# A SwiGLU feed-forward whose up products are formed as 7 half-size block products, with the down products in a stage of their own

## The chip, the cores and the metric

The kernel runs on 1 core of one Trainium2 chip. The metric is the device time of one execution in microseconds (us). The time before is 2326.37 us, the median of 3 runs (2324.08, 2326.37 and 2328.72).

## What is computed

One layer of a hybrid encoder on 1152 tokens (1024 of a prompt, 128 of 8 running streams): retention and differential attention, merged and projected, and then a feed-forward with a residual. The change touches the feed-forward and the stages just ahead of it:

```python
h = h + merged @ W_o
x2 = rmsnorm(h, norm2_g)
g, u = split(x2 @ w_ffn_up)          # 1024 -> 2 x 2816
h = h + (silu(g) * u) @ w_ffn_down   # 2816 -> 1024
y = rmsnorm(h, normf_g)
```

All values are float32. The kernel splits each operand of a product into a high part h, rounded by a cast, and a low part l, the difference, and sums three products, high x high, high x low and low x high (`mm3`, L82).

## The kernel before

Tokens are held in 9 blocks of 128, in three tiles of 384. The feature axis of 1024 has 8 slices of 128 (`KT`). The last stages are these.

- The branch product (`pdb`, weights w_db) writes the merged vector as MH and ML, three tiles each.
- The output projection `proj(b, half)` (tiles `pe`, 24 matmuls of 512 columns) adds the residual into H, which stays in SBUF for all 9 blocks. `norm2(b)` forms the norm, and `turn2()` transposes it (tiles `pte`) into X2H and X2L.
- The feed-forward runs over 22 slices f of 128 hidden features. `split_w` (L188) loads one block of weights (512 KB), casts the high part on ScalarE and forms the low part on VectorE, each 128x512 or 128x1024. `ffn_dense` (L1277) makes 24 matmuls of 384 columns for each of the three token tiles: 72 for a gate block (`pg`), 72 for an up block (`pu`). ScalarE applies Silu to the gate (L1291); VectorE multiplies the up product into it (L1374), ScalarE casts (L1375) and GpSimd forms the low part (L1376).
- After each pair of slices, `down(fs_, acts, final)` makes 12 matmuls of 512 columns for each of 9 token blocks (`pd`, two halves, two slices): 108 matmuls. VectorE adds each result into H (L1393). The last call also forms the final norm and stores the output.

Every load and store is issued by SyncE (`load` L73, `store` L76), in the order of its queue. The instructions of one engine run in the order in which the program lists them; the order around the feed-forward comes from the tile framework's scheduling of this code.

```python
for p_ in range(NF // 2):
    pair = (2 * p_, 2 * p_ + 1)
    last = p_ == NF // 2 - 1
    acts = [up(pair[0])]
    if last:
        down(*prev, False)
    acts.append(up(pair[1]))
    if prev is not None and not last:
        down(*prev, False)
    prev = (pair, acts)
```

Of the kernel before, what the change touches and what calls it, by code (L numbers as in the profile page):

```python
# [19 lines left out]
P = 128  # L20
# [10 lines left out]
KT = 8  # L31
# [31 lines left out]
def tile_kernel(ctx, tc, I, O):  # L63
# [15 lines left out]
    def mm(out, l, r, start, stop):  # L79
        nc.tensor.matmul(out, l, r, start=start, stop=stop)  # L80
# [8 lines left out]
    wp = pool(ctx, "wp", 2)  # L89
# [122 lines left out]
    vecd = dr.tile([DH, VL], F, name="vecd", tag="vecd")  # L212
    skd = [dr.tile([P * (VL + 1)], F, name=f"skd{h}", tag=f"skd{h}") for h in range(DH)]
# [1004 lines left out]
    xstack.close()  # L1218


    mstack = ExitStack()
    mp = pool(mstack, "mp", 3)
    MH = [mp.tile([P, KT, 384], R, name=f"MH{c}", tag="MH") for c in range(3)]
    ML = [mp.tile([P, KT, 384], R, name=f"ML{c}", tag="ML") for c in range(3)]
    wo0 = ExitStack()
    wop = pool(wo0, "wo0", 1)

    def split_w_o(pool_, half, kp, raw_pool=None):
        raw = (raw_pool or wp).tile([P, 1024], F, name=f"wo{half}{kp}w", tag="wr", bufs=1)
# [8 lines left out]
    wo_0 = []  # L1238
    with ExitStack() as st:
        yp = pool(st, "dy", 1, None, "right")  # L1240
        tp = pool(st, "dt", 4, None, "right")
        YD = [[yp.tile([P, KT, 384], R, name=f"YD{i}{c}", tag=f"YD{i}{c}") for c in range(3)] for i in range(2)]
        for c in range(3):
            load_split(YD[0][c], YD[1][c], yd[c])
        for n in range(KT):
            w = split_w(wp, I["w_db"][n], f"db{n}")
            for c in range(3):
# [10 lines left out]

                def evac(c, ps):
                    nc.vector.tensor_tensor(gt, ps, gt, op=ALU.mult)  # L1260
                    nc.gpsimd.tensor_tensor(mt, mt, gt, op=ALU.add)  # L1261

                for _ in dense_c(w, YD, c, 0, evac, f"pdb{n}"):
                    pass
                nc.scalar.copy(MH[c][:, n, :], mt)
                nc.vector.tensor_tensor(ML[c][:, n, :], mt, MH[c][:, n, :].bitcast(F), op=ALU.subtract)
            if n >= KT - 4:
                wo_0.append(split_w_o(wop, 0, n - KT + 4, tp))


    hstack = ExitStack()
    hp = pool(hstack, "hp", 1, None, "right")
    H = hp.tile([P, 9, 1024], F, name="H", tag="H")
    fs = pool(hstack, "fs", 2, None, "right")
    X2H, X2L = [None] * 3, [None] * 3

    def ffn_dense(w, evac, name):  # L1277
        h, l = w
        for c in range(3):
            ps = psum("dq", f"{name}_{c}")  # L1280
            for k in range(KT):
# [12 lines left out]
    with ExitStack() as st:  # L1294
        wo1 = pool(st, "wo1", 1, None, "right")
        ep = pool(st, "ep", 2, None, "right")
        g2 = ep.tile([P, 1024], F, name="g2", tag="g2", bufs=1)
        load(g2, I["norm2_g"].broadcast_to([P, 1024]))
        wo = (wo_0, [split_w_o(wo1, 1, kp) for kp in range(4)])
        w_g0 = split_w(wp, I["w_up"][0], "wg0")  # L1300

        def proj(b, half):
            c, j = b // 3, b % 3
# [3 lines left out]
            load(xt, I["x_all"][r0:r1, hs])  # L1307
            ps = psum("m", f"pe{b}_{half}")
            for k in range(KT):
                h, l = wo[half][k // 2]  # L1310
                a = slice(j * P, (j + 1) * P)
                mh, ml = MH[c][:, k, a], ML[c][:, k, a]
                mm(ps, mh, h[:, k % 2, :], k == 0, False)
                mm(ps, mh, l[:, k % 2, :], False, False)
                mm(ps, ml, h[:, k % 2, :], False, k == KT - 1)
            nc.vector.tensor_tensor(H[:, b, hs], ps, xt, op=ALU.add)
# [3 lines left out]
        def norm2(b):  # L1320
            c = b // 3
            if b % 3 == 0:
                X2H[c] = mp.tile([P, KT, 384], R, name=f"X2H{c}", tag="MH")
                X2L[c] = mp.tile([P, KT, 384], R, name=f"X2L{c}", tag="ML")
            turns.append(norm_to_T(ep, H[:, b, :], b, P, g2, X2H[c], X2L[c], (b % 3) * P, "e"))
# [209 lines left out]
```

## Time and profile before

| what | value |
|---|---|
| median of the runs | 2326.37 us |
| the profiled execution | 2326.88 us |
| its span, first to last instruction | 2325.0 us |
| TensorE busy | 2288.9 us, 98% |
| VectorE busy | 968.5 us, 42% |
| ScalarE busy | 762.6 us, 33% |
| GpSimd busy | 502.9 us, 22% |
| moved by DMA | 200.01 MB, mean 86 GB/s |
| mean granted clock of TensorE | 0.998 of 2.4 GHz |

The profile shows one execution. Busy time of an engine off the chain costs nothing by itself; the chain that ended last shows which work set the end. PE is TensorE, DVE VectorE, ACT ScalarE, POOL GpSimd and SP SyncE.

### The profile page before, as it was taken

What the parts mean: (1) busy time and instruction counts of PE and PEld (TensorE: products, weight loads), DVE (VectorE), ACT (ScalarE), POOL (GpSimd) and SP (SyncE); (2) the same over time, 40 slices, a digit from 0 to 9 for tenths busy, and PEclk for the clock granted to TensorE, in tenths of its full rate; (3) what the DMA queues carried; (4) which work ended last, traced back from release to release, by engine and by line L of the source; (5) the groups of instructions that cost most, each with busy time, mean ns of one, the idle gap of its engine ahead of it and who ended that gap; (6) DMA issues with size and microseconds to landing.
All of it is one profiled execution on the core that took longest, in us unless ns stands there. A gap on an engine that the chain in (4) does not pass through costs nothing.

```text
span 2325.0 us, 34635 instructions
## 1 busy us (share of the span) xinstructions
PE 2288.9 (98%) x13738; PEld 2186.9 (94%) x13738; DVE 968.5 (42%) x2248; ACT 762.6 (33%) x1756; POOL 502.9 (22%) x591
## 2 busy tenths in 40 slices
PE   8999999999999999999999999999999999999998
PEld 8999999999999999999899998899999999999987
DVE  5353333434556555654442433323323342233345
ACT  4233223134555555555544322221121112111112
POOL 2132212133323332332434320010100011000101
PEclk9999999999999999999999999999999999999999
DMA  6422322234233232322428532111110111101112
GB/s 213 129 85 70 105 73 96 85 100 145 77 91 91 79 98 88 96 80 88 138 89 265 160 119 93 37 37 46 55 46 31 42 46 55 36 29 46 55 37 91
DMA packets 129362, 200.01 MB, mean 86 GB/s; under 512 B 13432, under 2 KB 97656, under 8 KB 129200
## 3 DMA queue, kind: packets, MB, share of 16 engines
q1 hardware_dynamic: 129200, 197.80, 27.1%
q8 instruction: 108, 1.77, 0.3%
q14 instruction: 54, 0.44, 0.1%
HBM read 148.76 MB, written 53.78 MB: 87 GB/s over the span
## 4 chain that ended last, share of the span: by engine, by line
PE 90%; DVE 4%; DMA 2%; ACT 2%; issue 1%; POOL 1%; SPq 0%; DVEq 0%; POOLq 0%; ACTq 0%
PE pu L80 12%; PE pg L80 12%; PE pd L80 11%; PE ddv L80 4%; PE ddk L80 4%; PE pdb L80 4%; PE pe L80 4%; PE drv L80 4%; PE dgd L80 4%; PE dgr L80 4%; PE drg L80 4%; PE ddq L80 3%; PE po L80 3%; PE psc L80 3%; PE drb L80 3%; PE drk L80 2%
## 5 line engine op out<-in xcount | busy, mean ns | idle before, releaser
L1376 POOL TENSOR_TENSOR afl<-sgf,afh 128x384 fp32r<-128x384 f32 x66 | 70.1, 1062 | 729.8 <-ACT afh L1375 729.8
L1393 DVE TENSOR_TENSOR H<-pd,H 128x512 f32<-128x512 f32 x198 | 136.2, 690 | 109.6 <-PE pd L80 109.6
L915 DVE CUSTOM_DVE_ANT_0 E<-psc,TB 128x144 f32<-128x144 f32 (+6 forms) x224 | 113.0, 507 | 112.5 <-PE psc L80 106.3
L1291 ACT ACTIVATE sgf<-pg 128x384 f32<-128x384 f32 x66 | 32.3, 489 | 313.9 <-PE pg L80 313.9
L894 ACT ACTIVATE E<-E,ng 128x272 f32<-128x272 f32 (+7 forms) x128 | 101.0, 789 | 47.1 <-DVE ng L920 44.0
L1374 DVE TENSOR_TENSOR sgf<-pu,sgf 128x384 f32<-128x384 f32 x66 | 36.7, 556 | 169.1 <-PE pu L80 169.1
L80 PE MATMUL psc<-K,QH 128*128 128x144 f32 (+6 forms) x224 | 73.3, 330 | 6.9 <-DVE mx L915 5.2
L1375 ACT CAST afh<-sgf 128x384 fp32r<-128x384 f32 x66 | 33.7, 511 | 117.0 <-DVE sgf L1374 116.9
L80 PE MATMUL psc<-K,QL 128*128 128x144 f32 (+6 forms) x224 | 71.1, 319 | 0.0
L975 DVE TENSOR_TENSOR al<-pa,ah 128x512 fp32r<-128x512 f32 (+1 forms) x80 | 46.4, 582 | 43.8 <-ACT ah L974 42.9
L904 DVE SCALAR_TENSOR_TENSOR E<-E,rt,E 128x144 f32<-128x144 f32 (+3 forms) x64 | 54.7, 855 | 0.0
L80 PEld LDWEIGHTS psc<-K,QH 128*128 128x128 f32 x224 | 42.2, 188 | 10.4 <-issue 5.5
L566 POOL TENSOR_TENSOR v<-V,v 128x256 fp32r<-128x256 f32 x36 | 27.0, 749 | 113.4 <-ACT v L565 113.4
L792 DVE SCALAR_TENSOR_TENSOR QL<-ddq,QH 64x384 fp32r<-64x384 f32 (+1 forms) x48 | 24.5, 510 | 57.5 <-ACT QH L786 54.9
L974 ACT CAST ah<-pa 128x512 fp32r<-128x512 f32 (+1 forms) x80 | 40.2, 503 | 23.5 <-PE pa L963 23.2
L963 PE MATMUL pa<-ident,E 128*128 128x128 f32 x288 | 44.6, 272 | 0.0
L1261 POOL TENSOR_TENSOR mt<-mt,gt 128x384 f32<-128x384 f32 x24 | 24.4, 1017 | 83.0 <-DVE gt L1260 70.4
L80 PEld LDWEIGHTS psc<-K,QL 128*128 128x128 f32 x224 | 42.3, 189 | 0.0
L532 ACT COPY V<-drv 128x256 f32<-128x256 f32 x36 | 13.4, 372 | 83.9 <-PE drv L80 83.9
L80 PE MATMUL po<-al,VH 128*128 128x256 f32 x128 | 36.4, 284 | 1.8 <-DVE al L975 1.7
L963 PEld LDWEIGHTS pa<-ident,E 128*128 128x128 f32 x288 | 35.1, 140 | 2.2
L620 POOL TENSOR_TENSOR Sp<-S,Sp 128x256 fp32r<-128x256 f32 x32 | 23.9, 747 | 60.1 <-ACT Sp L619 52.2
(1774 smaller groups left out, 8064.7 us busy)
## 6 DMA issues: line engine op xcount, KB each, us to landing
skd<-vecd SPq DMA_DIRECT2D x8, 584.0 KB, 13.0
out_k_t<-kf SPq DMA_DIRECT2D x8, 584.0 KB, 3.3
xt<-in_x_all SPq DMA_DIRECT2D x9, 512.0 KB, 5.4
vd<-v SPq DMA_DIRECT2D x36, 128.0 KB, 1.7
yr<-SG SPq DMA_DIRECT2D x24, 192.0 KB, 1.8
gd<-gdt SPq DMA_DIRECT2D x24, 192.0 KB, 1.8
gr<-grt SPq DMA_DIRECT2D x24, 192.0 KB, 1.8
YRL<-yr SPq DMA_DIRECT2D x12, 384.0 KB, 5.0
```

What stands on the lines that cost most here:

```text
L80: nc.tensor.matmul(out, l, r, start=start, stop=stop)
L894: nc.scalar.activation(E[m][:, :nk], E[m][:, :nk], AF.Exp, bias=ng[:, m : m + 1], accum_out=sm[:, m : m + 1])
L904: nc.vector.scalar_tensor_tensor(E[0][:, :nk], E[1][:, :nk], rt[:, 0:1], E[0][:, :nk], op0=ALU.mult, op1=ALU.add)
L915: nc.vector.tensor_tensor_reduce(out=E[m][:, k0:k1], in0=ps, in1=TB[:, u0 : u0 + k1 - k0], scale=1.0, scalar=-3e38, op0=ALU.add, op1=ALU.m ...
L963: nc.tensor.transpose(pt[:, o : o + P], blk[2 * g + j][:, NM + P * t : NM + P * (t + 1)], ident)
L974: nc.scalar.copy(ah[:, :o], pt[:, :o])
L975: G.later(LAT["ah"], lambda ah=ah, al=al, pt=pt, o=o: nc.vector.tensor_tensor(al[:, :o], pt[:, :o], ah[:, :o].bitcast(F), op=ALU.subtract))
L1291: nc.scalar.activation(sg[:, 384 * c : 384 * (c + 1)], ps, AF.Silu)
L1374: nc.vector.tensor_tensor(sg[:, cs], ps, sg[:, cs], op=ALU.mult)
L1375: nc.scalar.copy(ah[:, cs], sg[:, cs])
L1376: nc.gpsimd.tensor_tensor(al[:, cs], sg[:, cs], ah[:, cs].bitcast(F), op=ALU.subtract)
L1393: nc.vector.tensor_tensor(H[:, b, hs], ps, H[:, b, hs], op=ALU.add)
```

## The change

**Gate and up products.** The weights w_up are taken in 22 groups of two blocks, with the features in two halves k (512 each) and the tokens in two halves t (576 each). The first group (gate of slices 0 and 1) is formed as before, by `dense_gate`, 72 matmuls of 384 columns for each block. In the other 21 groups, the 2x2 block product over (two weight blocks) x (two halves of k) x (two halves of t) is formed from 7 products in place of 8. A product is 4 slices x 3 matmuls for each of two column ranges of 288. The products are taken in the order 1, 6, 2, 7, 5, 4, 3. The sums of weight blocks for products 5, 6, 7 and 3 (S) are made by GpSimd, and their high and low parts by ScalarE and VectorE (`w_group`, `halves`). The sums of token operands for products 7, 5, 6 and 4 (T, high and low, 4 slices x 576) are made once, in three thirds of 4 x 192 elements, after the last transpose. The results are put together in PSUM and in `s1`, `U2` and `U3`.

**Activations and H through DRAM.** The finished activations of two slices are stored to `actd`, and H to `hd`; both are read back later.

**Down products.** They are a stage of their own: three passes over three token blocks. In a pass, 6 PSUM banks hold the sums over all 22 slices; each slice loads its w_down block (512 KB) and 128x384 activations (192 KB), casts and splits them, and makes 18 matmuls of 512 columns. H is read back and added at the end of a pass. In the last pass the three last slices are taken block by block.

**Around it.** MH and ML are one tile each, and take the transposed norm as well. The weights of the branch product are split in 512-wide halves, from a pool of 8 buffers with two raw buffers.

```diff
+    hd = [dr.tile([P, 1024], F, name=f"hd{b}", tag=f"hd{b}") for b in range(9)]
+    actd = [dr.tile([P, NTOK], F, name=f"act{f}", tag=f"act{f}") for f in range(NF)]
...
+    ORDER = "1627543"
...
+            sums = {
+                "6": ((s1, a21, a22, ALU.add), (s2, s1, a11, ALU.subtract)),
+                "7": ((s3, a11, a21, ALU.subtract),), "3": ((s4, a12, s2, ALU.subtract),),
+            }
+            src = {"1": a11, "2": a12, "4": a22, "5": s1, "6": s2, "7": s3, "3": s4}
+            for p in ORDER:
+                for o, a, b, op in sums.get(p, ()):
+                    nc.gpsimd.tensor_tensor(o, a, b, op=op)
+                (W[p],) = halves(src[p], f"wu{g}_{p}", None, 1)
+                yield
...
+            key = {"1": "A", "2": "A", "6": "B", "7": "D", "4": "D", "5": "C", "3": "C"}[p]
+            s_ = st_[c]
+            new = key not in s_
+            if new:
+                s_[key] = fpsum(f"{name}{key}{c}")[:, :288]
+            ps, (ah, al), (bh, bl) = s_[key], W[p], XO[p]
+            cs = slice(288 * c, 288 * (c + 1))
+            for k in range(4):
                 ks = slice(k * P, (k + 1) * P)
-                mm3(ps[:, :384], h[:, ks], l[:, ks], X2H[c][:, k, :], X2L[c][:, k, :], k == 0, k == KT - 1)
-            evac(c, ps[:, :384])
-            yield
-
-    def gate_f(f, w):
-        sg = fs.tile([P, NTOK], F, name=f"sgf{f}", tag="sgf")
-
-        def ev_g(c, ps):
-            nc.scalar.activation(sg[:, 384 * c : 384 * (c + 1)], ps, AF.Silu)
-        return sg, ffn_dense(w, ev_g, f"pg{f}")
-
-    with ExitStack() as st:
-        wo1 = pool(st, "wo1", 1, None, "right")
-        ep = pool(st, "ep", 2, None, "right")
+                mm(ps, ah[:, ks], bh[:, k, cs], new and k == 0, False, not new)
+                mm(ps, al[:, ks], bh[:, k, cs], False, False, not new)
+                mm(ps, ah[:, ks], bl[:, k, cs], False, k == 3, not new)
...
+            if p == "1":
+                s_["s1"] = tmp("s1")
+                nc.scalar.copy(s_["s1"], ps)
+            elif p == "2":
+                evac(0, 0, c, ps, None)
+            elif p == "6":
+                s_["U2"] = tmp("U2")
+                nc.vector.tensor_tensor(s_["U2"], ps, s_["s1"], op=ALU.add)
+            elif p == "7":
+                s_["U3"] = tmp("U3")
+                nc.vector.tensor_tensor(s_["U3"], ps, s_["U2"], op=ALU.add)
+            elif p == "5":
+                evac(1, 1, c, ps, s_["U3"])
+            elif p == "4":
+                evac(1, 0, c, ps, s_["U2"])
+            else:
+                evac(0, 1, c, ps, s_["U2"])
...
+    dense_gate(0, 0)
+    turn2()
+    dense_gate(0, 1)
+    dense_gate(0, 2)
...
+            def out(p, eng):
+                h, l = (a[:, :, cs] for a in T[p])
+                nc.scalar.copy(h, t[p])
+                sub(l, t[p], h.bitcast(F), eng)
+            def between(p, a, b, eng):
+                t[p], d = new("d"), new("e")
+                sub(t[p], a[0], b[0], eng)
+                sub(d, a[1], b[1], eng)
+                sub(t[p], t[p], d, eng, ALU.add)
+            def less(p, a, u, eng):
+                t[p] = new("f")
+                sub(t[p], a[0], u, eng)
+                sub(t[p], t[p], a[1], eng, ALU.add)
+            between("5", x[0, 1], x[0, 0], nc.gpsimd)
+            less("6", x[1, 1], t["5"], nc.vector)
+            out("6", nc.vector)
+            out("5", nc.vector)
+            between("7", x[1, 1], x[0, 1], nc.gpsimd)
+            out("7", nc.vector)
+            t6 = t["6"]
+            t["4"] = t6
+            sub(t["4"], x[1, 0][0], t6, nc.vector)
+            sub(t["4"], t["4"], x[1, 0][1], nc.vector, ALU.add)
+            out("4", nc.vector)
...
+    Wg, st_g = w_group(NF // 2)
+    for n in range(2):
+        for c in range(3):
+            if n:
+                dense_gate(n, c)
+                next(st_g, None)
...
+    def ev_up(n, t, c, ps, u):
+        o = sg[n][:, 576 * t + 288 * c : 576 * t + 288 * (c + 1)]
+        if u is None:
+            nc.vector.tensor_tensor(o, ps, o, op=ALU.mult)
+        else:
+            v = up_.tile([P, 288], F, name=f"v{n}{t}{c}", tag="v", bufs=2)
+            nc.vector.tensor_tensor(v, ps, u, op=ALU.add)
+            nc.gpsimd.tensor_tensor(o, v, o, op=ALU.mult)
...
+    def w_down(p_, f):
+        w = halves(raw_w(I["w_down"][f], f"wd{p_}_{f}"), f"wd{p_}_{f}")
+        raw = fp.tile([P, 384], F, name=f"ar{p_}_{f}", tag="ar", bufs=2)
+        load(raw, actd[f][:, 384 * p_ : 384 * (p_ + 1)])
+        ah = fp.tile([P, 384], R, name=f"ah{p_}_{f}", tag="ah")
+        al = fp.tile([P, 384], R, name=f"al{p_}_{f}", tag="al")
+        nc.scalar.copy(ah, raw)
+        nc.gpsimd.tensor_tensor(al, raw, ah.bitcast(F), op=ALU.subtract)
+        return w, ah, al
...
+        strassen(W, XO, ev_up if u else ev_gate, nxt, f"f{i}")
+        if u:
+            for n in range(2):
+                store(actd[2 * p_ + n], sg[n])
...
-            def ev_u(c, ps):
-                cs = slice(384 * c, 384 * (c + 1))
-                nc.vector.tensor_tensor(sg[:, cs], ps, sg[:, cs], op=ALU.mult)
-                nc.scalar.copy(ah[:, cs], sg[:, cs])
-                nc.gpsimd.tensor_tensor(al[:, cs], sg[:, cs], ah[:, cs].bitcast(F), op=ALU.subtract)
...
+        for p_ in range(3):
+            ps = {(b, half): fpsum(f"pd{p_}_{b}_{half}") for b in range(3) for half in range(2)}
+            hr = []
+            for b in range(3):
+                hr.append(yp.tile([P, 1024], F, name=f"hr{p_}_{b}", tag="hr", bufs=4))
+                load(hr[b], hd[3 * p_ + b])
+            def block(b, f, w, ah, al):
                 bs = slice(b * P, (b + 1) * P)
                 for half in range(2):
+                    (wh, wl), o = w[half], ps[b, half]
+                    mm(o, ah[:, bs], wh, f == 0, False)
+                    mm(o, ah[:, bs], wl, False, False)
+                    mm(o, al[:, bs], wh, False, f == NF - 1)
+            ops = w_down(p_, 0)
+            late = []
+            for f in range(NF):
+                now = ops
+                if f + 1 < NF:
+                    ops = w_down(p_, f + 1)
+                if p_ == 2 and f >= NF - 3:
+                    late.append((f, *now))
+                else:
+                    for b in range(3):
+                        block(b, f, *now)
...
-                    ps = psum(("m", "tr")[half], f"pd{fs_[0]}_{b}_{half}")
-                    for i, ((wh, wl), (ah, al)) in enumerate(zip(ws, acts)):
-                        mm(ps, ah[:, bs], wh[:, hs], i == 0, False)
-                        mm(ps, ah[:, bs], wl[:, hs], False, False)
-                        mm(ps, al[:, bs], wh[:, hs], False, i == len(ws) - 1)
-                    nc.vector.tensor_tensor(H[:, b, hs], ps, H[:, b, hs], op=ALU.add)
```

On GpSimd, between the last transposes and the first group of 7 products, the rows before are the low parts of activations (afl); those of the change are the sums of token operands. td and te are what T5 and T7 are formed in, S is a tile of weight sums, wu1 a pair of raw weight blocks, sg a gate tile.

```order
L114 TENSOR_TENSOR re7r<-re7t,mhalf 128x1
L114 TENSOR_TENSOR re8r<-re8t,mhalf 128x1
L1376 TENSOR_TENSOR afl_16642<-sgf_16483,afh_16641 128x384 x3
L1376 TENSOR_TENSOR afl_16821<-sgf_16741,afh_16820 128x384 x3
L1376 TENSOR_TENSOR afl_17000<-sgf_16920,afh_16999 128x384 x3
L1376 TENSOR_TENSOR afl_17179<-sgf_17099,afh_17178 128x384 x3
```

Now, same engine, from the second third of the sums to the first products of the first group (the six operations of a third stand ahead in the same pattern):

```order
L1465 TENSOR_TENSOR td_16762<-MH 128x768
L1465 TENSOR_TENSOR td_16762<-td_16762,te_16763 128x768
L1465 TENSOR_TENSOR te_16774<-ML 128x768
L1465 TENSOR_TENSOR td_16773<-MH 128x768
L1465 TENSOR_TENSOR td_16773<-td_16773,te_16774 128x768
L1465 TENSOR_TENSOR te_16786<-ML 128x768
L1322 TENSOR_TENSOR S_16949<-wu1bw 128x512
L1322 TENSOR_TENSOR S_16949<-wu1aw,wu1bw 128x512
L1322 TENSOR_TENSOR S_16949<-S_16949,wu1aw 128x512
L1322 TENSOR_TENSOR S_16949<-wu1aw,S_16949 128x512
L1465 TENSOR_TENSOR td_16785<-MH 128x768
L1465 TENSOR_TENSOR td_16785<-td_16785,te_16786 128x768
```

The four weight sums of the second group (S) have come to stand between the last T7 operation te and its td; all of this is new on GpSimd.

On VectorE at the same place, rows that did not exist before, up to the low part of the last third of T6 (last row; T_16629 is the low tile of T6, T_16627 of T5, T_16625 of T7, T_16631 of T4):

```order
L1465 TENSOR_TENSOR T_16629<-tf_16755,T_16628 128x4x192
L1465 TENSOR_TENSOR T_16625<-td_16762,T_16624 128x4x192
L1465 TENSOR_TENSOR tf_16755<-MH,tf_16755 128x768
L1465 TENSOR_TENSOR tf_16755<-tf_16755,ML 128x768
L1236 TENSOR_TENSOR wu_3l_16909<-S_16827,wu_3h_16908 128x512
L1465 TENSOR_TENSOR T_16627<-td_16773,T_16626 128x4x192
L1465 TENSOR_TENSOR T_16631<-tf_16755,T_16630 128x4x192
L1236 TENSOR_TENSOR wu_1l_16951<-wu1aw,wu_1h_16950 128x512
L1465 TENSOR_TENSOR tf_16778<-MH,td_16773 128x768
L1465 TENSOR_TENSOR tf_16778<-tf_16778,ML 128x768
L1465 TENSOR_TENSOR T_16629<-tf_16778,T_16628 128x4x192
```

Each row waits for the one ahead, so the last T6 comes behind T7 and T4 of the second third and two weight differences.

On SyncE, the loads of the feed-forward before, in the stretch of slices 4 to 9 (wg and wu are blocks of w_up, wd of w_down):

```order
L74 DMA wd4w<-in_w_down 128x1024
L74 DMA wd5w<-in_w_down 128x1024
L74 DMA wg8w<-in_w_up 128x1024
L74 DMA wu8w<-in_w_up 128x1024
L74 DMA wg9w<-in_w_up 128x1024
L74 DMA wu9w<-in_w_up 128x1024
```

And in the first down pass of the change (ar is the activation tile):

```order
L74 DMA ar_17_22594<-act_189 128x384
L74 DMA wd_18w<-in_w_down 128x1024
L74 DMA ar_18_22628<-act_190 128x384
L74 DMA wd_19w<-in_w_down 128x1024
L74 DMA ar_19_22662<-act_191 128x384
L74 DMA wd_20w<-in_w_down 128x1024
```

One w_down block and one activation tile stand for each slice, in each of three passes; before, each w_down block was loaded once, among four blocks of w_up a pair.

## Rows read from the trace of the kernel before

**Rows 1.** The page: span, busy time of TensorE, and the chain by line.
```profile
span 2325.0 us, 34635 instructions
PE 2288.9 (98%) x13738; PEld 2186.9 (94%) x13738; DVE 968.5 (42%) x2248; ACT 762.6 (33%) x1756; POOL 502.9 (22%) x591
...
PE pu L80 12%; PE pg L80 12%; PE pd L80 11%; PE ddv L80 4%; PE ddk L80 4%; PE pdb L80 4%; PE pe L80 4%; PE drv L80 4%; PE dgd L80 4%; PE dgr L80 4%; PE drg L80 4%; PE ddq L80 3%; PE po L80 3%; PE psc L80 3%; PE drb L80 3%; PE drk L80 2%
```

**Rows 2.** Chain of waits, feed-forward: start us, us, what, instructions.
```profile
1503.65 12.48 PE pu L80 x72
1516.13 12.48 PE pg L80 x72
...
1591.01 25.20 PE pd L80 x108
...
2292.35 4.21 PE pd L80 x18
```

**Rows 3.** Chain of waits: products of 400 and of 256 columns.
```profile
52.56 12.62 PE drk L80 x70
...
194.03 11.16 PE drv L80 x93
```

**Rows 4.** Waits of TensorE from 1400 us on.
```profile
PE pte L366 <- DVE X2L L369: 0.5, 1, 0.5
PE pg L80 <- DVE X2L L369: 0.4, 1, 0.4
```

**Rows 5.** Groups by line from 1100 us: shapes, count | busy us, mean ns.
```profile
L1376 POOL TENSOR_TENSOR afl<-sgf,afh 128x384 fp32r<-128x384 f32 x66 | 70.1, 1062 | 729.8 <-ACT afh L1375 729.8
...
L197 POOL TENSOR_TENSOR wgr7l<-wgr7w,wgr7h 128x512 fp32r<-128x512 f32 x2 | 2.6, 1282 | 3.9 <-issue 3.8
...
L1393 DVE TENSOR_TENSOR H<-pd,H 128x512 f32<-128x512 f32 x198 | 136.2, 690 | 109.6 <-PE pd L80 109.6
...
L368 ACT CAST X2H<-pte 128x512 fp32r<-128x512 f32 x18 | 9.7, 590 | 48.4 <-PE pte L366 48.4
```

**Rows 6.** Timeline of VectorE from 1224 us: start, us, instruction.
```profile
1226.43 1.22 DVE L1138 TENSOR_TENSOR YD<-YD,YD 128x768 fp32r<-128x768 f32 x1 [2.42 <-ACT YD L1137]
...
1231.72 0.96 DVE L1138 TENSOR_TENSOR YD<-YD,YD 128x768 fp32r<-128x768 f32 x1 [3.60 <-ACT YD L1137]
...
1245.24 1.90 DVE L1138 TENSOR_TENSOR YD<-YD,YD 128x768 fp32r<-128x768 f32 x1 [3.23 <-ACT YD L1137]
...
1249.46 0.96 DVE L1138 TENSOR_TENSOR YD<-YD,YD 128x768 fp32r<-128x768 f32 x1 [1.85 <-ACT YD L1137]
```

**Rows 7.** Timeline of GpSimd in the same stretch.
```profile
1225.00 1.84 POOL L1138 TENSOR_TENSOR YD<-YD,YD 128x768 fp32r<-128x768 f32 x1 [6.38 <-ACT YD L1137]
...
1232.70 1.85 POOL L1138 TENSOR_TENSOR YD<-YD,YD 128x768 fp32r<-128x768 f32 x1 [0.84 <-ACT YD L1137]
...
1244.53 1.80 POOL L1138 TENSOR_TENSOR YD<-YD,YD 128x768 fp32r<-128x768 f32 x1 [3.32 <-PE drb L80]
...
1249.48 2.65 POOL L1138 TENSOR_TENSOR YD<-YD,YD 128x768 fp32r<-128x768 f32 x1
```

**Rows 8.** TensorE after 1244 us: timeline; window (busy us, PEclk, DMA share, GB/s).
```profile
1247.67 0.69 PE L80 MATMUL drb<-YRH,wrb5h 128*128 128x384 f32 x1 [3.19 <-DVE rbt L1164]
...
1250.67 0.35 PE L80 MATMUL drb<-YRH,wrb5h 128*128 128x384 f32 x1
...
1248.00:1250.00 2.00, 2.00 (x7) 2.00 (x7) 0.54 (x1) 0.83 (x1) 2.00 (x3) 0.50 0.65 202
```

**Rows 9.** DMA issues (KB each, median us to landing), and windows as in 8.
```profile
xt<-in_x_all SPq DMA_DIRECT2D x9, 512.0 KB, 5.4
...
wd0w<-in_w_down SPq DMA_DIRECT2D x1, 512.0 KB, 3.3
...
1220.00:1240.00 20.00, 19.96 (x116) 19.64 (x115) 5.44 (x7) 8.72 (x13) 8.77 (x6) 1.00 0.92 302
...
1487.00:2292.00 805.00, 804.11 (x4272) 754.64 (x4272) 266.34 (x385) 135.18 (x208) 70.18 (x67) 1.00 0.14 42
```

More of the change, by code (lines that the diff above doesn't have):

```diff
@@ L1218, in tile_kernel, with halves, raw_w, split_w_o @@
     xstack.close()
-    mstack = ExitStack()
[L1222 to L1229, printed above, removed]
+    wstack.close()
+    rstack = ExitStack()
+    rp = pool(rstack, "rp", 8, None, "right")
+    def halves(raw, name, eng=None, parts=2):
+        out = []
+        for i in range(parts):
+            cs = slice(512 * i, 512 * (i + 1))
+            h = rp.tile([P, 512], R, name=f"{name}h{i}", tag="h")
+            l = rp.tile([P, 512], R, name=f"{name}l{i}", tag="l")
+            nc.scalar.copy(h, raw[:, cs])
+            (eng or nc.vector).tensor_tensor(l, raw[:, cs], h.bitcast(F), op=ALU.subtract)
+            out.append((h, l))
+        return out
+    def raw_w(src, name):
+        raw = rp.tile([P, 1024], F, name=name + "w", tag="wr", bufs=2)
+        load(raw, src)
+        return raw
+    mstack = ExitStack()
+    mp = pool(mstack, "mp", 1)
+    MH = mp.tile([P, KT, NTOK], R, name="MH", tag="MH")
+    ML = mp.tile([P, KT, NTOK], R, name="ML", tag="ML")
+    wos = ExitStack()
+    def split_w_o(pool_, half, kp):
+        raw = rp.tile([P, 1024], F, name=f"wo{half}{kp}w", tag="wr", bufs=2)
         load(raw, I["w_o"][half, kp])
@@ new lines, in tile_kernel, with w_group, steps @@
+    ORDER = "1627543"
+    def w_group(g):
+        W = {}
+        def steps():
+            r0 = raw_w(I["w_up"][2 * g], f"wu{g}a")
+            r1 = raw_w(I["w_up"][2 * g + 1], f"wu{g}b")
+            S = sp.tile([P, 4, 512], F, name=f"S{g}", tag="S")
+            a11, a12, a21, a22 = r0[:, :512], r0[:, 512:], r1[:, :512], r1[:, 512:]
+            s1, s2, s3, s4 = (S[:, i, :] for i in range(4))
+            sums = {
[8 more added lines that the diff above has]
+                yield
+        return W, steps()
@@ L1297, in tile_kernel, with fpsum @@
+    ring = ["m", "dq", "tr", "o", "m", "dq", "tr", "tr"]
+    turn_ = [0]
+    def fpsum(name):
+        t = ring[turn_[0] % 8]
+        turn_[0] += 1
+        return psum(t, name)
+    fstack = ExitStack()
+    sstack = ExitStack()
+    sp = pool(sstack, "sp", 1, None, "right")
+    sg = [None, None]
+    with wos:
+        wop1 = pool(wos, "wo1", 1)
+        ep = pool(wos, "ep", 2)
         g2 = ep.tile([P, 1024], F, name="g2", tag="g2", bufs=1)
         load(g2, I["norm2_g"].broadcast_to([P, 1024]))
-        wo = (wo_0, [split_w_o(wo1, 1, kp) for kp in range(4)])
@@ L1300, in tile_kernel @@
-        w_g0 = split_w(wp, I["w_up"][0], "wg0")
+        wo[0].append(split_w_o(wop1, 0, 3))
+        wo[1] = [split_w_o(wop1, 1, kp) for kp in range(4)]
+        H = {}
         def proj(b, half):
-            c, j = b // 3, b % 3
             xt = ep.tile([P, 512], F, name=f"xe{b}_{half}", tag="xe")
@@ new lines, in tile_kernel, with dense_gate @@
+            if b + 3 < 9:
+                proj(b + 3, 0)
+        w_c = [halves(raw_w(I["w_up"][n], f"wc{n}"), f"wc{n}") for n in range(2)]
+    up_ = pool(fstack, "up", 1)
+    xc = pool(fstack, "xc", 1)
+    sg = [up_.tile([P, NTOK], F, name=f"sg0_{n}", tag=f"sg{n}") for n in range(2)]
+    T = {p: [xc.tile([P, 4, 576], R, name=f"T{p}{i}", tag=f"T{p}{i}") for i in range(2)] for p in "7564"}
+    def dense_gate(n, c):
+        ps = fpsum(f"pg{n}_{c}")[:, :384]
+        cs = slice(384 * c, 384 * (c + 1))
+        for k in range(KT):
+            h, l = w_c[n][k // 4]
+            ks = slice((k % 4) * P, (k % 4 + 1) * P)
+            mm3(ps, h[:, ks], l[:, ks], MH[:, k, cs], ML[:, k, cs], k == 0, k == KT - 1)
+        nc.scalar.activation(sg[n][:, cs], ps, AF.Silu)
@@ L1410, in tile_kernel @@
-        prev = None
-        for p_ in range(NF // 2):
-            pair = (2 * p_, 2 * p_ + 1)
-            last = p_ == NF // 2 - 1
-            acts = [up(pair[0])]
-            if last:
-                down(*prev, False)
-            acts.append(up(pair[1]))
-            if prev is not None and not last:
-                down(*prev, False)
-            prev = (pair, acts)
-        down(*prev, True)
-    hstack.close()
+                    (wh, wl), o = w[half], ps[b, half]
+                    mm(o, ah[:, bs], wh, f == 0, False)
@@ L1423, in tile_kernel @@
+    sstack.close()
     mstack.close()
+    rstack.close()
 _OUTS = {
```

196 lines of the change are left out of this document (107 added, 89 removed).

## The prediction

> **What bounds the kernel now.** I read the page first. The span is 2325.0 us and TensorE is busy for 98% of it; by line, the chain that ended last holds the gate products (pg), the up products (pu) and the down products (pd) with 12, 12 and 11% [rows 1]. The reader is to see that these three are one long stretch of matmuls. The chain of waits shows how it is built: blocks of 72 matmuls of 384 columns take 12.48 us each, one per block of w_up, and 108 matmuls of 512 columns take 25.20 us, one per pair of w_down blocks [rows 2]. The waits of TensorE from 1400 us to the end sum to 0.9 us [rows 4]. So whatever takes matmul columns away here shortens the kernel, as long as the other engines and the loads keep up.
>
> The profiled execution took 2326.88 us, 1.9 more than its span and 0.5 above the median of the runs, 2326.37. The sum is made against 2326.9.
>
> **Fewer columns.** Two weight blocks (w_up has 44) cost 2 x 12.48 = 24.96 us. One pair stays dense; the other 21 pairs become 7 products x 2 halves x 12 matmuls = 168 matmuls of 288 columns. The trace has no 288. The nearest rows are 256 columns, 11.16 / 93 = 120.0 ns, and 384 columns, 12.48 / 72 = 173.3 ns [rows 2, 3]; these are the ends. The row of 400 columns, 12.62 / 70 = 180.3 ns, and the 512-column one, 25.20 / 108 = 233.3 ns, lie near one line with them, 0.42 to 0.47 ns a column, so I take 133.3 ns, on the line. A pair then costs 168 x 133.3 = 22.40 us and saves 2.56; 21 pairs save 53.8 us. At 120 ns they would save 101, at 173.3 they would lose 87.
>
> The Trainium skill (TensorE: Matmul & The Clock Gate, "Wait — 56ns, not 53.3ns?") has a column at 1/2.4 ns and about 2.5 ns fixed per matmul. By it 384 columns would take 162.5 ns, which the 173.3 of this trace contradicts, and the saving would be an estimated 59 us; the row decides.
>
> **The down products** keep their 1188 matmuls of 512 columns, 11 x 25.20 = 277.2 us, so nothing is gained or lost on TensorE. They now run in three passes of 22 steps, 18 matmuls or 4.20 us each, and each step loads 512 KB of w_down and 192 KB of activations. The cover for these loads: 704 KB in 4.2 us is 168 GB/s, while the 20 us from 1220 moved 302 GB/s [rows 9]. With two raw buffers, one load (3.3 us) and its readers (two casts of 0.59 us, two differences of 0.69 us [rows 5]) take 3.3 + 2.5 = 5.8 us, or 2.9 a step: below 4.2, costed at nothing. If the cover goes, the price is in the second rival.
>
> **Work beside the products.** An up group needs 4 sums of 512 on GpSimd (5.2 us at 1.28), 7 casts on ScalarE (4), 7 differences (4.8) and a dozen evacuations of 288 columns on VectorE (scaled from 0.69 for 512, 0.45 each, 5.4), and 6 products of 288 on GpSimd (about 0.8 each from 1.06 for 384, 4.8). VectorE has 10 and GpSimd 10 of 22.4 us. Even if they never worked side by side, 20 us fit. I cost this at nothing; the third rival is its price. Loads and stores: 22 stores of 576 KB and 9 of 512 KB, 17 MB, are new before the down passes, over some 560 us, so 31 GB/s beside the 42 GB/s that this stretch moved at a DMA share of 0.14 [rows 9]; they wait on SyncE's queue for finished tiles, and the loads of a group stand a group ahead of its use. Nothing.
>
> **The first group.** Here I expect a stall. The operand sums T5, T6, T7 and T4 are formed in thirds of 768 elements, from the last transpose on, by GpSimd (two differences and a sum for T5, the same for T7) and VectorE (T6, T4, and every low part), with casts on ScalarE between. TensorE's cover from that transpose: five dense thirds of 4.16 us, 20.8; product 1, 24 x 0.133 = 3.2; product 6, first half, 1.6. That is 25.6 us. Product 6, second half, needs the last third of T6.
>
> The order lists what stands ahead of that: 16 GpSimd operations of 768 and 4 weight sums of 512, and 20 VectorE operations of 768 with 4 differences of 512. Alone, a 768 takes 1.85 us on GpSimd and 0.96 on VectorE [rows 6, 7]. When both want to run, the rows show them taking turns: the VectorE operation begun at 1245.24 inside GpSimd's (until 1246.33) ended at 1247.14, 0.81 after it; that of 1226.43 ended 0.81 after GpSimd's; and GpSimd's of 1249.48, begun beside VectorE's, lasted 2.65 instead of 1.85 [rows 6, 7]. The Trainium skill (SBUF — State Buffer, "SBUF: two separate sides") says the same as a rule: the port pair of the two is locked for a whole instruction when VectorE has two SBUF inputs. By the rule this change's sums, put on both engines to share them, gain almost nothing from it.
>
> Taking turns: GpSimd 16 x 1.85 + 4 x 1.28 = 34.7; VectorE, each after a wait, 20 x 0.81 + 4 x 0.6 = 18.6; together 53.3 us. Against 25.6 us of cover, TensorE stands still for 27.7, which I round to 28 for the handing over between engines. The lower bound is the chain without turns: GpSimd's 15 operations to the last T5 (27.8), then VectorE twice, a cast, VectorE (3.7), plus up to 6 for the five times that GpSimd must wait until a cast (0.83, scaled from 0.59 for 512) and a difference have emptied its buffer: 31.5 to 37.5 us, a stall of 6 to 12. The upper bound is turns at full length, 34.7 + 20 x 0.96 + 4 x 0.69 = 56.7, a stall of 31, and a few us for casts that nothing covers.
>
> After a stand of 3.5 us at 1244 the granted clock was at the lower level, 0.50 of 2.4 GHz, until about 1250.7 [rows 8]: 9 matmuls took 3.0 us instead of 1.6. One restart counts here, the one that ends the stall: 1.4 us.
>
> **The end.** The last down block now ends three steps of one token block at a time, so VectorE has no backlog when TensorE finishes. Of the 7.4 us after the last matmul (2292.35 + 25.20 = 2317.55 to 2325.0) I take off 1. The waits of 0.9 us before the gate products stay: block 8's norm chain has about as little cover as before.
>
> **Sum.** 2326.9 - 53.8 + 28 + 1.4 - 1 = 2301.5, less 0.5 for the median: **2301 us**.
>
> **The rivals.**
> 1. *No turns.* The sums overlap, since only eight or so operations in the trace show the turns, all near other traffic. The stall is 6 to 12, say 10: 2283. Against it: the rows of 1226, 1245 and 1249 agree to 0.01 us. Chance 0.19.
> 2. *The down steps are paced by loads* (the slower side). Place: the 66 steps; mechanism: two raw buffers, so a step lasts (load + 2.5) / 2. At 3.3 us a load is far off, but loads of the same 512 KB took 5.4 us where many transfers ran [rows 9], and here each goes beside a load of small rows. It shows from 5.9 us a load; the 25 us of net gain are gone at 66 x 0.38, a load of 6.7. At 7.0 us: 66 x 0.55 = 36, 2337 us. Chance 0.10.
> 3. *The groups lose time to their neighbours.* Each of the 21 groups waits for a bank, a weight difference or a GpSimd sum; 20 us of taking turns in 22.4 leaves little for lateness. 0.5 us a group gives 2312, 1 us 2322. Chance 0.15.
> 4. *A 288-column matmul costs less*, 125 ns: 168 x 21 x 8.3 ns = 29 us less, 2272. Chance 0.04.
>
> **How the numbers follow.** The forecast has 0.52, with its own range of 2294 to 2309 (stall 21 to 36). The range is 2281 to 2323: it takes in the first rival and the third up to 1 us a group, and leaves out the second, the fourth and the worst of the third, some 0.18. A measurement of this kernel tells about 0.2%, 4.7 us, from no change. Faster by more (below 2321.7): the forecast, rivals 1 and 4, and most of 3: 0.52 + 0.19 + 0.04 + 0.09 = 0.84. Within it: 0.04 of rival 3. Slower: rival 2 and a rest of 3, 0.12.
>
> **What would show it.** Right: blocks of 168 matmuls at 22.4 us in the chain; one stretch of some 25 to 30 us before the first group's product 6, in two waits, released by T6, with GpSimd and VectorE never both at normal length in it; a granted clock of 0.5 for a few us behind it; 4.2 us a step in the down passes with no waits. Wrong: waits of TensorE for w_down or activation tiles at every step; waits of about equal length in all 21 groups; a stall below 15; or matmuls of 288 columns whose starts are not 133 ns apart.

## The result and the profile after

The change takes 2302.67 us (median of 4 runs, 2300.27 to 2303.84) against 2327.39 for the kernel before beside it (4 runs); the ratio is 0.9895, 95% interval 0.9877 to 0.9912. It is faster by 24.7 us. The forecast was 2301 us, range 2281 to 2323.

The page of the changed kernel, three lines, against [rows 1]:

```profile
span 2300.0 us, 37117 instructions
...
PE 2233.9 (97%) x14242; PEld 2137.5 (93%) x14242; DVE 1100.1 (48%) x2409; ACT 885.2 (38%) x2055; POOL 723.2 (31%) x759
...
PEclk8999999999999999999999999979999999999999
```

TensorE is busy 55 us less, yet the span fell by only 25; the one 7 in the row of the clock marks the place. The chain of waits of the changed kernel (start us, us, what, instructions), against [rows 2]:

```profile
1496.70 4.17 PE pg L80 x24
...
1555.45 2.77 PE f0B L80 x10
1558.22 4.00 PE f0A L80 x24
...
1578.22 3.20 PE f1B L80 x24
...
2019.94 3.20 PE f20C L80 x24
2023.14 260.47 PE pd L80 x1149
```

From f1 on, a product is 24 matmuls in 3.20 us, 133.3 ns each, and a group is 22.40 us; the down products run without a gap, at 260.47 / 1149 = 226.7 ns. Only the first group (f0) stands out. The waits of TensorE from 1370 us on, in the same trace, show why:

```profile
PE f0B L80 <- ACT T L1477: 23.6, 2, 18.0
PE f0B L80 <- DVE T L1465: 1.6, 2, 0.8
```

Product 6 (f0B) waits 25.2 us for the sums of token operands: T's high part is cast on ScalarE, its low part formed on VectorE. The two spans compared by stage, each from where TensorE begins it:

| stage | before, us | after, us | difference |
|---|---|---|---|
| up to the branch product (pdb) | 1282.4 | 1284.6 | +2.2 |
| pdb and projection, to the first gate block | 204.7 | 212.1 | +7.4 |
| gate and up products (down products left out) | 553.3 | 526.4 | -26.9 |
| down products | 277.2 | 269.3 | -7.9 |
| after the last matmul | 7.4 | 7.6 | +0.2 |

The last two rows use 2023.14 + 1188 x 0.2267 = 2292.4 us as the end of the down products. The code of the first stage is the same in both kernels; its 2.2 us is within what differed there from one profiled kernel of this study to the next (its last part, drb, began between 1156.6 and 1162.1 us). Two of the nine batches of transposes (pte, 0.87 us each) stand ahead of the first gate block in the change and behind it in the kernel before, so 1.7 us of the third row's gain are only moved there from the second row.

### The profile page after: what moved, and what is told of

Same layout as the page of the kernel before. It is cut to its first block, busy times and chain, and to the rows that moved or that the text cites. A ratio compares the mean times of both kernels' runs of the same rounds, so it can differ in the third digit from the quotient of the medians.

```text
span 2300.0 us, 37117 instructions
## 1 busy us (share of the span) xinstructions
PE 2233.9 (97%) x14242; PEld 2137.5 (93%) x14242; DVE 1100.1 (48%) x2409; ACT 885.2 (38%) x2055; POOL 723.2 (31%) x759
## 5 line engine op out<-in xcount | busy, mean ns | idle before, releaser
L1538 POOL TENSOR_TENSOR al<-ar,ah 128x384 fp32r<-128x384 f32 x66 | 75.4, 1144 | 189.6 <-ACT ah L1537 183.7
L1529 POOL TENSOR_TENSOR sg<-v,sg 128x288 f32<-128x288 f32 x66 | 62.0, 939 | 163.1 <-DVE v L1528 129.5
L1236 DVE TENSOR_TENSOR wu_6l<-S,wu_6h 128x512 fp32r<-128x512 f32 x21 | 22.0, 1047 | 52.7 <-ACT wu_6h L1235 50.1
L1537 ACT CAST ah<-ar 128x384 fp32r<-128x384 f32 x66 | 33.6, 509 | 26.8 <-DMA ar<-act 15.9
L1520 ACT ACTIVATE sg<-sg 128x288 f32<-128x288 f32 x60 | 26.6, 443 | 37.3 <-DVE sg L1519 37.3
L794 POOL CAST QH<-QH 64x384 fp32r<-64x384 f32 (+1 forms) x48 | 22.4, 467 | 54.6 <-ACT QH L788 52.3
L767 POOL TENSOR_TENSOR K<-kf,K 64x400 fp32r<-64x400 f32 (+2 forms) x24 | 27.8, 1160 | 36.1 <-ACT K L764 35.8
```

Of the source, the lines that this page charges most:

```text
L767: lambda: nc.gpsimd.tensor_tensor(K[64:128, 0, lo:hi], kf[0:64, lo:hi], K[0:64, 0, lo:hi].bitcast(F), op=ALU.subtract),
L1529: nc.gpsimd.tensor_tensor(o, v, o, op=ALU.mult)
L1537: nc.scalar.copy(ah, raw)
L1538: nc.gpsimd.tensor_tensor(al, raw, ah.bitcast(F), op=ALU.subtract)
```

## The experiments

**What the first group's wait costs: leave the sums out.**

```diff
-    XO.update(T)
+    XO.update({"7": X[1, 1], "5": X[0, 1], "6": X[1, 0], "4": X[0, 0]})
...
-            between("5", x[0, 1], x[0, 0], nc.gpsimd)
...
-            out("4", nc.vector)
```

> Leaves out the sums of token operands (T): products 7, 5, 6 and 4 read plain quarters of the transposed norm instead, so the feed-forward's values are other ones; every matmul, weight sum, evacuation, load and store stays. Theory A (the whole loss at the first group is the wait for T): the two waits before product 6, 25.2 us in the trace of the change, and the slow restart behind them (lower clock until 1559.4, some 2.5 us) go, and nothing takes their place: about 2302.7 - 27.7 = 2275 us, no wait of TensorE over 1 us from 1500 us on. Rival B (the weight sums and splits of the first groups, or banks, are late as well and only hidden behind T): a wait of 5 us or more stays at the first or second group, 2280 or above.

Measured: 2273.63 us, 29.0 less than the change, and no wait of TensorE behind 1495 us. Its chain of waits:

```profile
1498.20 4.17 PE pg L80 x24
...
1503.33 20.81 PE pg L80 x120
1524.14 3.20 PE f0A L80 x24
1527.34 3.20 PE f0B L80 x24
...
1994.56 260.47 PE pd L80 x1149
```

f0B follows f0A at once. From the first gate block (1498.20) to the down products it takes 496.36 us, the change 526.44: the sums cost 30.1 us, and nothing else was late behind them. Theory A holds.

**Why the sums take so long: all of them on VectorE.**

```diff
-            between("5", x[0, 1], x[0, 0], nc.gpsimd)
+            between("5", x[0, 1], x[0, 0], nc.vector)
...
-            between("7", x[1, 1], x[0, 1], nc.gpsimd)
+            between("7", x[1, 1], x[0, 1], nc.vector)
```

> All sums of token operands on VectorE, in the order of before; GpSimd keeps the weight sums. Theory A (GpSimd and VectorE take turns at SBUF, so an operation moved from GpSimd to VectorE shortens the line by the difference of their times, 1.85 to 0.96): up to the last third of T6 16 x 0.89 = 14 us less, minus the waits for casts that now lie open (some 9 casts of 0.83 us, half of them hidden): 8 to 13 us less, 2290 to 2295 us. Rival B (the two engines work side by side and the time goes into the chain of dependences and casts): moving 16 operations onto the other engine's queue gains nothing or costs up to 10 us, 2303 to 2313.

Measured: 2288.70 us in one run, 14.0 less than the change, one more than the range of theory A. From the first matmul of the gate blocks to the first of the down products it is 513.8 us against 526.5, 12.7 less. The waits of TensorE behind 1490 us in this kernel:

```profile
PE f0B L80 <- ACT T L1477: 13.8, 1, 13.8
...
PE f0B L80 <- DVE T L1465: 0.9, 1, 0.9
```

25.2 us of waits became 14.7 by giving one engine the work of two. In the trace of the change the turns can be read off directly. GpSimd, from the timeline (start us, us, instruction, idle before):

```profile
1503.77 1.85 POOL L1465 TENSOR_TENSOR te<-ML 128x768 f32<-128x768 f32 x1
...
1507.63 2.62 POOL L1465 TENSOR_TENSOR te<-ML 128x768 f32<-128x768 f32 x1
1511.14 2.50 POOL L1465 TENSOR_TENSOR td<-MH 128x768 f32<-128x768 f32 x1 [0.90 <-DVE T L1465]
1513.73 2.44 POOL L1465 TENSOR_TENSOR td<-td,te 128x768 f32<-128x768 f32 x1
1516.25 1.85 POOL L1465 TENSOR_TENSOR te<-ML 128x768 f32<-128x768 f32 x1
```

And VectorE in the same stretch:

```profile
1508.46 2.60 DVE L1465 TENSOR_TENSOR T<-td,T 128x768 fp32r<-128x768 f32 x1
1510.99 0.95 DVE L1465 TENSOR_TENSOR tf<-tf,ML 128x768 f32<-128x768 f32 x1
1512.84 1.62 DVE L1465 TENSOR_TENSOR T<-tf,T 128x768 fp32r<-128x768 f32 x1 [0.91 <-ACT T L1477]
```

The same operation takes 1.85 us or up to 2.6 on GpSimd, 0.95 or 1.6 to 2.6 on VectorE. So it is not only that GpSimd is the slower engine: 11 of its 16 operations for the sums ahead of the last T6 took 2.14 us or more. VectorE's of 1508.46 began inside GpSimd's of 1507.63 (to 1510.25) and ended 0.81 us after it, the figure that [rows 6, 7] gave. The Trainium skill (SBUF — State Buffer, "SBUF: two separate sides") states that whichever of the two starts first keeps the shared port pair for its whole instruction and the other waits, where VectorE has two inputs in SBUF. Every such pair in this stretch agrees; the one place where VectorE read one input from PSUM (two differences for ML at 1502.05, 1.29 us together) ran beside GpSimd with neither made longer.

**More cover: one more dense group.** Two up blocks dense, the loop over groups begins one later.

```diff
-    Wg, st_g = w_group(NF // 2)
+    w_u = [halves(raw_w(I["w_up"][NF + n], f"wv{n}"), f"wv{n}") for n in range(2)]
+    for c in range(3):
+        dense_gate(1, c)
...
+    Wg, st_g = w_group(1)
     for n in range(2):
         for c in range(3):
-            if n:
-                dense_gate(n, c)
-                next(st_g, None)
+            dense_up(n, c)
+            next(st_g, None)
+        store(actd[n], sg[n])
...
-    G2 = [(p_, u) for p_ in range(NF // 2) for u in range(2)][1:]
+    G2 = [(p_, u) for p_ in range(NF // 2) for u in range(2)][2:]
```

> The change with the up blocks of the first two slices dense as well, so that product 6 is first needed 24.96 us later; 20 of 22 groups are formed from 7 products. Theory A (the sums need 53.6 us from the last transpose by their turns, 5 fewer here as the second group's weight sums no longer stand in between, and the cover grows from 25.6 to 50.6): the wait shrinks from 25.2 us to 0 to 3, the slow restart goes, 2.56 us of saving are given up: 2302.7 - 30.2 + 2.6 + 0 to 3 = 2275 to 2278 us. Rival B (what the first group waits for is given by its own weights and sums and comes along with it to wherever the first group stands): a wait of 15 us or more stays, 2290 to 2305.

Measured: 2290.22 us (2285.38 to 2291.52), ratio to before 0.9825, interval 0.9802 to 0.9849. Faster than the change, but by 12 us and not 25. Theory A misses; the time lies in the range of rival B, but not by its mechanism. The waits from 1495 us on:

```profile
PE f0A L80 <- ACT f0s L1351: 6.5, 1, 6.5
PE f0B L80 <- DVE sg L1515: 5.2, 1, 5.2
```

The wait for T is gone, and 11.7 us of new ones took its place. The 5.2 us are for a bank: the dense up products are read out by VectorE (L1515), and these readings stand in its queue behind the sums. VectorE's timeline in this kernel:

```profile
1550.39 0.55 DVE L1515 TENSOR_TENSOR sg<-pu,sg 128x384 f32<-128x384 f32 x1
...
1558.31 0.55 DVE L1515 TENSOR_TENSOR sg<-pu,sg 128x384 f32<-128x384 f32 x1
```

The first up products were formed from 1524 us on; the first of them was read at 1550. The 6.5 us are for ScalarE's copy of product 1 (f0s), which has to be done before product 2 is added in the same bank. ScalarE's timeline:

```profile
1566.82 0.51 ACT L1550 CAST ah<-ar 128x384 fp32r<-128x384 f32 x1 [6.51 <-DMA ar<-act]
...
1568.27 0.69 ACT L1351 COPY f0s<-f0A 128x288 f32<-128x288 f32 x2
```

In its queue the copy stands behind a cast for the down products (ah), and this waits for activations that are stored and loaded again only when VectorE has read out the up products: the third reading ended at 1561.32, the store was issued at 1561.35, the load at 1564.43. So both waits go back to VectorE, one through a bank and one through a store, a load and another engine's queue. I had counted what TensorE would do meanwhile, and not who empties its banks.

**Both at once.** The two edits above in one kernel.

> The edits of the two kernels before in one: up blocks of the first two slices dense, and all token sums on VectorE. Theory A (the wait is covered by the dense blocks already): within 3 us of the kernel with dense blocks alone, 2273 to 2277. Rival B: two gains that add, another 10 us less, 2265.

Measured: 2274.53 us in one run, and no wait behind 1490 us. Within the range of theory A as a number, though by another way than it said: against the dense group alone it is 16 us, since VectorE comes to its readings earlier (the first of them at 1529.89 us, not 1550.39). From the first gate block to the down products it takes 2.5 us more than the kernel without sums, which is the saving that one more dense group gives up; so nothing of the sums' cost is left.

**The down products: where does 226.7 ns come from?** The kernel before holds both lengths. Its projection, TensorE's timeline, first half (weights wo0) and second half (wo1):

```profile
1400.40 0.39 PE L80 MATMUL pe<-wo01h,ML 128*128 128x512 f32 x1
1400.63 0.39 PE L80 MATMUL pe<-wo01h,MH 128*128 128x512 f32 x1
...
1424.24 0.40 PE L80 MATMUL pe<-wo12l,MH 128*128 128x512 f32 x1
1424.47 0.40 PE L80 MATMUL pe<-wo12h,ML 128*128 128x512 f32 x1
1424.71 0.40 PE L80 MATMUL pe<-wo13h,MH 128*128 128x512 f32 x1
```

From start to start 0.227 us in the first half (226.9 ns in the mean) and 0.23 to 0.24 in the second (233.3), with the same stationary tiles. The place of the streamed weights in SBUF differs. Three kernels move the down weights of the kernel before, the first by letting them change places with the activations, the others by unused bytes ahead of them:

```diff
-        fp = pool(st, "fp", 2)
         wd = pool(st, "wd", 2)
+        fp = pool(st, "fp", 2)
```

> The kernel before with one edit: the pool of the down weights is opened ahead of the pool of activations, so that the two change places in SBUF (weights from byte 96,000 of a partition instead of 153,536). Theory A (the 512-column matmul takes 226.7 or 233.3 ns depending on where its streamed operand lies: in the kernel before, the projection's first half, from 96,000, took 226.7 and its second half, from 150,496, 233.3): the down blocks go from 25.20 to 24.5 us, 7.8 us less, 2318.5 to 2319.5 us. Rival B (the down matmul is shorter because six banks are filled over 22 slices instead of one over two): 25.20 us a block, 2326 to 2327.

```diff
+        pad = pool(st, "pad", 1).tile([P, 464], F, name="pad", tag="pad")
+        nc.gpsimd.memset(pad, 0.0)
         wd = pool(st, "wd", 2)
```

> The kernel before with 1856 unused bytes a partition ahead of the down weights, so that they start at byte 155,392, which has the same remainder by 2048 as 96,000, where the matmuls took 226.7 to 227.0 ns. Theory A (the region of the partition matters, not the alignment in 2048 bytes): 25.20 us a block as before, 2326 to 2328. Rival B (the alignment matters): 24.5 us a block, 2319 to 2322.

The third has `[P, 8]` in place of `[P, 464]`.

> The kernel before with 32 unused bytes a partition ahead of the down weights: they start at byte 153,568, whose remainder by 2048 is 2016, that of the down weights in the change; the activations stay at remainder 256 by 512. Theory A (what counts is how streamed and stationary operand lie to each other: equal remainder by 512, or a smaller power of two, takes 226.7 ns, another 233.3): 233.3 ns, 25.20 us a block, 2326 to 2328. Rival B (the remainder of the streamed operand alone counts, and 1792 and 2016 are good ones): 227 ns, 2319 to 2322.

Their chains, one down block each, in this order:

```profile
1593.16 24.52 PE pd L80 x108
```

```profile
1590.29 24.52 PE pd L80 x108
```

```profile
1596.87 25.19 PE pd L80 x108
```

2322.39, 2319.55 and 2333.09 us, one run each; the first and the third are 3 and 5 us above what the theory that held had given. The stages ahead, alike in these kernels, make most of that (the first gate block begins 2.2 and 5.9 us later than in the kernel before). From the first gate block to the last matmul the three take 823.4, 823.4 and 830.8 us, the kernel before 830.7. So the place of the weights is worth 7.3 of the 7.9 us, and neither six banks nor the long sums are needed for it; the other 0.6 was not looked into. For the region of the partition (theory A of the second kernel) the answer is no: 155,392 is as good as 96,000. The third shows that the streamed operand's own remainder does not decide either: 2016 by 2048 is fast in the change and slow here. What is left is one rule that fits all the cases I have (addresses as the built kernels have them): fast where the streamed and the stationary tile begin at the same remainder by 512 bytes in the partition (256 and 256 in the first two, in the projection's first half and in both halves of the change's projection, at 226.8 to 227.3 ns; 480 and 480 in the change's down products), slow where not (448 against 256 in the down products of the kernel before, 480 against 256 in its projection's second half and in the third). The rule had been written down ahead of the third kernel alone, which came out as it says; otherwise it is a fit to these places. By how small a power of two they must agree, and whether it holds elsewhere, is open; 192 bytes of difference is already slow.

**All blocks dense, the rest of the change kept.**

```diff
-    W = Wg
-    G2 = [(p_, u) for p_ in range(NF // 2) for u in range(2)][1:]
+    for i, blk in enumerate(blocks):
+        u, f = divmod(blk, NF)
...
+                mm3(ps, h[:, ks], l[:, ks], MH[:, k, cs], ML[:, k, cs], k == 0, k == KT - 1)
```

> All 44 gate and up blocks dense (72 matmuls of 384 columns each), no sums, everything else as in the change: down products a stage of their own, activations and H through DRAM. Theory A (7 products save 53.8 us of matmuls and pay 27.7 at the first group; the rest of the change is worth -7.8 in the down products by shorter matmuls, +5 in the branch product, +2 in the projection): 2302.7 + 53.8 - 27.7 = 2329 us, blocks of 12.5 us and down matmuls at 226.7 ns. Rival B (the shorter down matmuls come with the half-size products or what stands around them in memory): down matmuls at 233.3 ns, 2337.

Measured: 2324.04 us. Its chain of waits:

```profile
1495.33 4.17 PE pg L80 x24
...
1500.46 544.97 PE pg L80 x3144
2045.42 260.47 PE pd L80 x1149
```

The gate and up blocks take 2045.42 - 1495.33 = 550.1 us. Against the kernel without sums, 496.4, that is 53.7: the price of the eighth product, as forecast. The down products keep their 226.7 ns, so rival B is out. Theory A's total was 5 us high, in a single run; 2.4 of that is the sums' cost, which it had at 27.7 instead of 30.1, and 1.4 the stages ahead (the first gate block begins at 1495.33, in the change at 1496.70).

**How near the down passes are to their loads.**

```diff
                 if f + 1 < NF:
                     ops = w_down(p_, f + 1)
+                    extra = yp.tile([P, 512], F, name=f"ax{p_}_{f}", tag="ax", bufs=2)
+                    load(extra, I["w_down"][f + 1][:, :512])
```

> The change with 256 KB more loaded at every step of the down passes (first half of the same w_down block, into a buffer that nothing reads): 960 instead of 704 KB a step of 4.08 us, 235 instead of 172 GB/s. Theory A (the loads have room: in the trace of the change the low part of a weight block is ready 10 us ahead of its use in most steps, and 3 us at the start of a pass): no wait or a few us at the two pass boundaries, 2302 to 2308. Rival B (the down steps stand close to being paced by loads, which take 5.3 to 6.1 us there against room for 5.7): 0.5 us or more a step, 2335 or above.

Measured: 2308.89 us in one run, just above theory A's range. The waits of TensorE from 2020 us on:

```profile
PE pd L80 <- ACT ah L1537: 1.9, 1, 1.9
PE pd L80 <- POOL al L1538: 0.5, 1, 0.5
```

With 36% more traffic two waits appear, both at the sixth of the 22 steps of the second pass (2137.7 and 2139.0 us; the pass began at 2115.2), and none at any other step. The down products take 4.6 us more with them. The loads are not what paces the change.

**The waits of pdb.** The change's branch product has waits of 4.3 us that the kernel before does not have (3.2 to 4.3 in all kernels built on it). Two edits tried to remove them: the casts of w_o moved behind a later block,

```diff
...
                     if n >= KT - 3:
-                        wo[0].append(split_w_o(wop0, 0, n - KT + 3))
+                        cast = split_w_o(wop0, 0, n - KT + 3)
...
+                if c == 1 and n >= KT - 3:
+                    wo[0].append(cast())
```

> The change, but in the branch product's stage the casts of three w_o blocks stand one 384-token block later on ScalarE than their loads, instead of right behind them. Theory A (ScalarE waits 2.3 us and less for w_o to land, and the Sigmoid behind it holds up VectorE and the PSUM banks; 3.4 to 4.3 us of waits of pdb for gt): these waits fall below 1.5 us, 2299 to 2300.5. Rival B (the gate tiles come late because three instead of four buffers hold them): the same waits, 2302 to 2304.

and four buffers for gt (with two for g2t), in the kernel with both edits at the first group:

```diff
-                gt = tp.tile([P, 384], F, name=f"gt{n}_{c}", tag="gt")
+                gt = tp.tile([P, 384], F, name=f"gt{n}_{c}", tag="gt", bufs=4)
```

> Dense up blocks for the first two slices and all token sums on VectorE, and in the branch product's stage four buffers for the gate tiles gt instead of three (and two for g2t). Theory A (the 3.4 us of waits of pdb for gt come from three buffers: a load of 3 us is asked for only when the buffer is free): these waits fall below 1 us, 2270 to 2272 us. Rival B (they come from ScalarE's order, where casts of weights stand ahead of the Sigmoid): the waits stay, 2274 to 2276.

The first gave 2302.48 us and did not do what it was meant to: ScalarE still waits for wo01 to land, as its row shows, and the waits for gt stay (the row below it):

```profile
1334.91 1.05 ACT L1261 CAST wo01h<-wo01w 128x1024 fp32r<-128x1024 f32 x1 [2.07 <-DMA wo01w<-in_w_o]
...
PE pdb L80 <- DVE gt L1297: 3.3, 3, 1.5
```

So the first neither shows nor refutes its theory. The second left them at 3.2 us as well, so three buffers for gt were not the cause. What is, stays open.

As a whole that last kernel took 2274.54 us (2272.86 to 2276.77, 4 runs), ratio to before 0.9777, interval 0.9754 to 0.9801: 28 us faster than the change, and level with the kernel with both edits at the first group alone (2274.53). Its chain at the first group:

```profile
1521.28 24.96 PE pu L80 x144
1546.24 3.20 PE f0A L80 x24
1549.44 3.20 PE f0B L80 x24
```

## Why the prediction was right, point by point

- *Fewer columns.* Right to the digit: 133.3 ns for 288 columns, on the line between 256 and 384, and 53.7 us between the dense kernel and the one without sums, against 53.8. The row of gate and up products shows 3.3 us more than these 53.7 less 30.1: 1.7 are the moved transposes, 0.9 the waits of [rows 4], which were to stay and are gone, and 0.7 I did not separate. The Trainium skill (TensorE: Matmul & The Clock Gate, "Wait — 56ns, not 53.3ns?") has about 2.5 ns fixed for each matmul, by which an estimated 59 us would have been saved; the measured widths, 13.3 ns above columns / 2.4, decide against it.
- *Work beside the products, at nothing.* Right: none of the 20 later groups has a wait. The third rival is out.
- *The first group, 28 us of stall and 1.4 of slow restart.* 30.1 measured, by the mechanism named. The turns were put at 53.3 us from the last transpose; the last T6 ended at 1553.80 + 1.59 = 1555.4, 53.5 us after the transposes' end at 1501.85. That it comes so near has some luck in it: an operation of GpSimd that had to wait for one of VectorE ended about 1.7 us behind it and not 1.85, while a seventeenth (1552.05) came in ahead of the last T6. The waits sum to 25.2, less than 28, and the clock took more than 1.4. The windows of the change (TensorE, weight loads, VectorE, ScalarE, GpSimd busy, PEclk, DMA share, GB/s):

```profile
1540.00:1550.00 10.00, 0.00 (x0) 0.00 (x0) 9.65 (x6) 3.06 (x6) 9.92 (x5) 0.50 0.00 1
...
1558.00:1559.00 1.00, 1.00 (x6) 1.00 (x6) 1.00 (x2) 0.98 (x2) 0.00 (x0) 0.50 0.00 0
1559.00:1560.00 1.00, 1.00 (x6) 1.00 (x6) 1.00 (x2) 0.00 (x0) 0.00 (x0) 0.56 0.00 0
1560.00:1561.00 1.00, 1.00 (x10) 1.00 (x9) 1.00 (x3) 0.00 (x0) 0.00 (x0) 1.00 0.00 0
```

  TensorE started again at 1555.4 and was at the lower level until about 1559.9; the matmuls between the waits, from 1531.4 on, ran at it too. Waits and slow matmuls together are 30.1. "One restart counts" was the wrong part: 4.9 us, not 1.4. So here too two errors cancel, 2.8 us less of waiting and 3.5 more of slow clock. The first rival (no turns, a stall of 6 to 12) is out.
- *The down products, "nothing is gained or lost on TensorE".* Wrong: 7.9 us gained. The step that failed took 233.3 ns for the price of a 512-column matmul; it is the price at one placement (7.3 us of it, by the kernels that moved the weights). The rows at hand held the sign: 256, 384 and 400 columns all lie 13.3 to 13.7 ns above columns / 2.4, 512 lay 20 above.
- *Its loads, at nothing.* Right, though the loads took longer there than the 3.3 us that I reckoned with: 4.2 us for w_down's block 10 and 6.1 for block 6, medians of three. The second rival is out: even with 36% more traffic it shows at one step.
- *The branch product and the projection* were not in the sum at all, and lost 7.4 us: 5.4 in the branch product (4.3 of waits of pdb, and slower matmuls behind them) and 2.0 in the projection (1.7 of moved transposes, 1.0 of waits, less 1.4 by the shorter matmuls of its second half, and 0.7 that I did not separate). The edits of the change there (raw weights through two shared buffers, three gate buffers) were passed over as having no cost; which of them costs it is open.
- *The end, 1 us less.* Not found: 7.6 us against 7.4.

So 2301 against 2302.67 is closer than the steps deserve: -7.9 was missing on the one side, and on the other 5.7 (the 7.4 without the moved transposes) and the 2.2 of the first stage, and they cancel. To that extent the number is luck; its two large terms came by the mechanisms named.

## What to carry to other kernels

Price the sums that a product with fewer multiplications needs at its first use, where nothing is yet in flight to cover them, and put two-operand SBUF work on one of VectorE and GpSimd rather than on both if it forms one line. Cover made of more matmuls is worth what the engine that empties their banks has free: here these readings stood in the same queue as the work to be covered. And read a matmul's price from several widths: one that lies off the others' line is a sign of something that can be changed.

## What the runs showed that I had not expected

A matmul with 512 streamed float32 columns took 226.7 or 233.3 ns by where its two operands lie in SBUF, where 32 unused bytes ahead of the weights made no difference and 1856 won 7.3 us in 1188 matmuls (24.52 us a block of 108 against 25.20). With 384 columns no such difference showed: 173.4 ns in the kernel before, with both operands at remainder 256, and 173.3 in the dense kernel, with 256 against 480. And after some 20 us of nearly no matmuls TensorE's clock was at its lower level, 0.50 of 2.4 GHz, for 4.4 us behind the restart; after 3.2 us without any [rows 8] for about 3.
